# An encoder trunk on one core: lo weights by an accumulating transfer, transforms by time modulo 4, final norm by 128 tokens

## The chip, the cores and the metric

The kernel runs on one core of a Trainium2 chip. The metric is the device time of one execution in microseconds (us), given as the median of several runs. A profiled execution stands beside it: its span runs from the first to the last instruction that the profiler records, and all times of instructions below are from that one execution. Engines are TensorE (PE, with its weight loads as PEld), VectorE (DVE), ScalarE (ACT), GpSimd (POOL) and SyncE (SP), which here issues transfers only.

## What is computed

A trunk of two layers on 512 tokens of 1024 channels, in float32. Cut to what matters here:

```python
for i in range(DEPTH):                       # 2
    h = rmsnorm(x, norm_mix_g[i])
    p = h @ w_in[i]                          # 1024 -> 2176
    y_a = rglru_mixer(...)                   # 384 channels, linear recurrences
    y_b = window_attention(...)              # 384 channels, 6 heads
    h_fwd, h_bwd = hyena_filters(...)        # depends on the weights alone
    y_c = hyena_mixer(c_u, ...)              # 256 channels
    y = concat(rmsnorm(y_a), rmsnorm(y_b), rmsnorm(y_c))
    x = x + y @ w_out[i]
    x = x + relu(rmsnorm(x) @ w_up[i])**2 @ w_down[i]     # 1024 -> 4096 -> 1024
return rmsnorm(x, final_norm_g)

def hyena_mixer(u, ...):
    x0, x1, v = split(depthwise_conv(u))
    z = v * x1
    y = irfft(rfft(z, 2 * L) * rfft(filt_circ, 2 * L))[:L] + z * bias   # L = 512
    return y * x0
```

## The kernel before

**A planner writes the order.** The program is not emitted as it is written. `Plan.record` collects operations with their inputs and outputs; `Plan.schedule` then plays a list schedule with a cost for each operation, and `Plan.issue` emits each engine's instructions in the order that came out. An operation recorded on `nc.any` goes to VectorE or GpSimd, one recorded with `plan.either` to whichever of the named engines is free. Tiles come from pools with a fixed number of buffers (`wraw` 6, `whi` 3, `wlo` 3, `sp` 69, PSUM 7), and an operation is placed only when its tiles have buffers. Where TensorE would have nothing to do, `filler` puts in a small bf16 matmul on constants (written to the tile `wk`), of which nothing is read. As the emission is by a helper, most instructions bear line 456 or 1459, and rows are told apart by tiles.

**Weights.** All products of weights run as three float32r matmuls (`mm3`): a weight is split into a rounded part hi and the rest lo, and the activations likewise, and hi*hi, hi*lo and lo*hi are added. `emit_weight` (line 588) takes the weights in the order `wseq`: SP loads 512 KB into a raw buffer (`load`, line 553, which waits until the third weight before is split), and `split_weight` (line 542) makes hi by a rounding copy and lo by a subtraction on VectorE or GpSimd. `weight` (line 610) keeps LA = 2 weights ahead (4 for the down weights).

**Stages.** For each layer: the input projection by 17 tiles (`pin`), with the recurrence's gates, the attention's units and the transforms between them in the order of the script of the layer (`SCRIPTS`, line 30; numbers are input tiles, F the filters, G the gates, R and U the attention, H the Hyena mixer, S the scan, N and O the group norms and output projections); the output projection (`po`); then the MLP in 8 quads: four tiles of the up projection (`pu`, 24 matmuls each) and, one quad later, the down projection by seven products (`pX`, `pY`, `pZ`, 12 matmuls each), each followed by VectorE's update of x.

**Transforms.** Transforms of length 1024 are matmuls with tables of cosines and sines of half-integer frequencies, split by even and odd time. `load_trig` (line 734) loads six tables of 128x512 and splits each. `dft` (line 755) is 12 float32r matmuls of 256 columns; `filters` (line 765) calls it 4 times, and so does `hyena` (line 1121) for its signal; then come products by frequency (Y), sums (G, split into hi and lo) and the inverse, 48 float32r matmuls of 256 columns.

**End.** The final norm (line 1297) runs by halves of 256 tokens: mean square, power -1/2 on GpSimd, x scaled in place, 16 transposes (`fin`), eight scaled copies out of PSUM, and eight stores of 128 KB by SP.

Of the kernel before, what the change touches and what calls it, by code (L numbers as in the profile page):

```python
# [10 lines left out]
F32 = mybir.dt.float32  # L11
# [158 lines left out]
class Plan:  # L170
# [112 lines left out]
    def schedule(self):  # L283
# [31 lines left out]
        while pending:  # L315
            moved = True
            while moved:
                moved = False
                for e in engines:
# [76 lines left out]
                    if o.dma:  # L396
                        dma_free = max(dma_free, t + 1.0) + c
                        free_at[e] = t + 0.45
                        end = dma_free + 1.2
                    else:  # L400
                        end = t + c
                        free_at[e] = end
                    if LOCK and (e == "gpsimd" or e == "vector" and self.two_port(o)):
                        port_free = end
# [55 lines left out]
def encoder_kernel(ctx, tc, xT, w_in, w_out, w_up, w_down, gates, fw, par, trig, rope, decay, zemb, ident_d, maskb_d, yT):  # L460
# [81 lines left out]
    def split_weight(raw, n, c, hi, lo):  # L542
# [4 lines left out]
        nc.any.tensor_tensor(out=lo[:, :n], in0=raw[:, :n], in1=hi[:, :n].bitcast(F32), op=ALU.subtract)  # L547
# [40 lines left out]
    def emit_weight(key):  # L588
# [10 lines left out]
        else:  # L599
# [5 lines left out]
            out = split_weight(raw, 1024, 128 if kind in ("in", "up") else 512, wtile(whi, F32R, "wh"), wtile(wlo, F32R, "wl"))  # L605
# [4 lines left out]
    def weight(key):  # L610
        n = wseq.index(key)
        la = LA if key[0] != "down" else LA + 2
# [142 lines left out]
    def dft(tabs, src, out):  # L755

        th, tl = [t.rearrange("p (c k) -> p c k", c=2) for t in tabs]
        sh, sl = [t.rearrange("p (c k) -> p c k", c=2) for t in src]
        for kt in range(2):
            o = out[:, kt * 256:(kt + 1) * 256]  # L760
            for c in range(2):
                ks = slice(kt * 128, kt * 128 + 128)
                mm3(o, th[:, c, ks], tl[:, c, ks], sh[:, c, :], sl[:, c, :], c == 0, c == 1)

    def filters(i, tr):
# [15 lines left out]
        for par_ in range(2):  # L781
# [14 lines left out]
            hs.append(split(s, "hs"))  # L796
            hd.append(split(d, "hd"))
        H = {}
        for nm, tb, src in (("c", (0, 4), hs), ("s", (1, 5), hd)):
            pe = PMX("He")  # L800
            dft(tr[tb[0]], src[0], pe)
            e = Fs("e")
            nc.scalar.copy(out=e, in_=pe)
            po = PMX("Ho")
            dft(tr[tb[1]], src[1], po)
            for sg, op in (("+", ALU.add), ("-", ALU.subtract)):
                H[nm + sg] = Fs("H" + nm + ("p" if sg == "+" else "m"))
                nc.vector.tensor_tensor(out=H[nm + sg], in0=e, in1=po, op=op)
        return H
# [28 lines left out]
    nc.any.tensor_scalar(out=hbias, in0=pcols(_cols["ba"][0], _cols["bx"][1]), scalar1=0.5, scalar2=1.0, op0=ALU.mult, op1=ALU.mult)  # L838
    nc.any.tensor_scalar(out=nsink, in0=pcols(*_cols["sink"]), scalar1=-1.0, scalar2=1.0, op0=ALU.mult, op1=ALU.mult)
    nc.any.tensor_scalar(out=s_, in0=lam, scalar1=-1.0, scalar2=1.0, op0=ALU.mult, op1=ALU.mult)  # L840
    nc.vector.tensor_tensor(out=ex, in0=lam, in1=s_, op=ALU.min)
    act(ex, ex, AF.Exp)
    nc.any.tensor_scalar(out=s2, in0=ex, scalar1=2.0, scalar2=1.0, op0=ALU.add, op1=ALU.mult)
    nc.vector.reciprocal(out=s2, in_=s2)
    nc.any.tensor_tensor(out=s_, in0=ex, in1=s2, op=ALU.mult)
    nc.any.tensor_tensor(out=s2, in0=s_, in1=s_, op=ALU.mult)
    nc.any.memset(pl, 2.0 / 17.0)
    for q in range(7, -1, -1):
        nc.any.tensor_tensor(out=pl, in0=pl, in1=s2, op=ALU.mult)
        nc.any.tensor_scalar(out=pl, in0=pl, scalar1=2.0 / (2 * q + 1), scalar2=1.0, op0=ALU.add, op1=ALU.mult)  # L850
    nc.any.tensor_tensor(out=pl, in0=pl, in1=s_, op=ALU.mult)
    nc.vector.tensor_scalar(out=s_, in0=lam, scalar1=-1.0, scalar2=0.0, op0=ALU.mult, op1=ALU.max)
    nc.any.tensor_tensor(out=pl, in0=pl, in1=s_, op=ALU.add)
    nc.any.tensor_scalar(out=m4sp, in0=pl, scalar1=-4.0, scalar2=1.0, op0=ALU.mult, op1=ALU.mult)
    nc.any.tensor_scalar(out=p4sp, in0=pl, scalar1=4.0, scalar2=1.0, op0=ALU.mult, op1=ALU.mult)
# [8 lines left out]
    for i in range(DEPTH):  # L864
# [256 lines left out]
        def hyena(H, tr):  # L1121
# [5 lines left out]
            for par_ in range(2):  # L1127
                p = PMX("zt")
                for c in range(2):
                    for n in range(2):  # L1130
                        src = v[n].rearrange("p (c s two) -> p c two s", c=2, two=2)[:, c, par_, :]
                        nc.tensor.transpose(p[:, c * 256 + n * 128:c * 256 + n * 128 + 128], src, ident)
                zt.append(split(p, "zt"))
            X = {}
            for nm, tb in (("c", (0, 4)), ("s", (1, 5))):
                pe = PMX("Xe")
# [327 lines left out]
```

## Time and profile before

| | |
|---|---|
| median of 3 runs | 1119.79 us (1119.63 to 1120.64) |
| profiled execution, its own time | 1119.31 us |
| its span | 1117.5 us |
| instructions | 14124 |
| TensorE / VectorE / ScalarE / GpSimd busy | 99% / 81% / 53% / 20% |

The busy time of TensorE holds the fills of `wk`, and matmuls overlap: the duration of one is longer than the distance to the next. What a matmul costs in a full stream is the distance between starts.

### The profile page before, as it was taken

What the parts mean: (1) busy time and instruction counts of PE and PEld (TensorE: products, weight loads), DVE (VectorE), ACT (ScalarE), POOL (GpSimd) and SP (SyncE); (2) the same over time, 40 slices, a digit from 0 to 9 for tenths busy, and PEclk for the clock granted to TensorE, in tenths of its full rate; (3) what the DMA queues carried; (4) which work ended last, traced back from release to release, by engine and by line L of the source; (5) the groups of instructions that cost most, each with busy time, mean ns of one, the idle gap of its engine ahead of it and who ended that gap; (6) DMA issues with size and microseconds to landing.
All of it is one profiled execution on the core that took longest, in us unless ns stands there. A gap on an engine that the chain in (4) does not pass through costs nothing. (4 is left out here: it accounts for less than half of the span.)

```text
span 1117.5 us, 14124 instructions
## 1 busy us (share of the span) xinstructions
PE 1105.6 (99%) x5224; PEld 900.1 (81%) x5224; DVE 901.8 (81%) x1374; ACT 587.5 (53%) x958; POOL 229.1 (20%) x143
## 2 busy tenths in 40 slices
PE   9999999999999999999999999999999999999997
PEld 6688788888888688888888888788888888888886
DVE  8999996568797886886989899685597797797796
ACT  6477664365345454344456836644554455355444
POOL 0221422301011131100332242242010111011032
PEclk9999999999999999999999999999999999999999
DMA  9424201221442412422252221022232431341312
GB/s 346 178 76 151 76 1 38 77 95 38 132 132 71 151 57 94 133 75 96 75 185 89 75 75 58 7 70 95 76 98 69 135 116 55 132 132 53 118 57 76
DMA packets 35132, 107.90 MB, mean 97 GB/s; under 512 B 4150, under 2 KB 6710, under 8 KB 35064
## 3 DMA queue, kind: packets, MB, share of 16 engines
q1 hardware_dynamic: 35064, 107.01, 29.1%
q8 instruction: 41, 0.67, 0.2%
q14 instruction: 27, 0.22, 0.1%
HBM read 104.90 MB, written 2.10 MB: 96 GB/s over the span
## 5 line engine op out<-in xcount | busy, mean ns | idle before, releaser
L456 ACT CAST wh<-wr 128x1024 fp32r<-128x1024 f32 x197 | 207.4, 1054 | 347.7 <-PE pu L456 133.8
L456 DVE TENSOR_TENSOR wl<-wr,wh 128x1024 fp32r<-128x1024 f32 (+1 forms) x171 | 213.5, 1251 | 133.2 <-ACT wh L456 129.2
L456 PE MATMUL pu<-xgh,wh 128*128 128x512 f32 x512 | 199.4, 389 | 0.1
L456 PE MATMUL pu<-xgh,wl 128*128 128x512 f32 x512 | 199.4, 390 | 0.0
L456 PE MATMUL pu<-xgl,wh 128*128 128x512 f32 x512 | 199.3, 389 | 0.0
L456 POOL TENSOR_TENSOR wl<-wr,wh 128x1024 fp32r<-128x1024 f32 x56 | 135.5, 2421 | 248.6 <-ACT wh L456 205.9
L456 PEld LDWEIGHTS pu<-xgh,wl 128*128 128x128 f32 x512 | 96.1, 188 | 21.4 <-issue 1.6
L456 PEld LDWEIGHTS pu<-xgh,wh 128*128 128x128 f32 x512 | 96.1, 188 | 20.2 <-ACT xgh L456 0.5
L456 PEld LDWEIGHTS pu<-xgl,wh 128*128 128x128 f32 x512 | 96.1, 188 | 19.9
L456 PE MATMUL pin<-xgh,wl 128*128 128x512 f32 x272 | 107.2, 394 | 0.0
L456 PE MATMUL pin<-xgl,wh 128*128 128x512 f32 x272 | 107.1, 394 | 0.0
L456 PE MATMUL pin<-xgh,wh 128*128 128x512 f32 x272 | 107.1, 394 | 0.0
L456 POOL TENSOR_TENSOR s<-s,h 128x256 f32<-128x256 f32 x12 | 8.9, 743 | 397.3 <-ACT wh L456 388.4
L456 DVE TENSOR_TENSOR wr<-wr 128x1024 f32<-128x1024 f32 x61 | 72.8, 1218 | 0.0
L456 PEld LDWEIGHTS pin<-xgl,wh 128*128 128x128 f32 x272 | 51.1, 188 | 12.1 <-DVE xgl L456 1.9
L456 PEld LDWEIGHTS pin<-xgh,wh 128*128 128x128 f32 x272 | 51.1, 188 | 12.0 <-DVE wl L456 0.8
L456 PEld LDWEIGHTS pin<-xgh,wl 128*128 128x128 f32 x272 | 51.1, 188 | 11.7 <-issue 1.3
L456 DVE SCALAR_TENSOR_TENSOR x<-po,tr,x 128x512 f32<-128x512 f32 x48 | 35.2, 747 | 25.4 <-PE po L456 16.8
L456 PE MATMUL po<-wh,ygh 128*128 128x512 f32 x128 | 51.6, 403 | 0.0
L456 PE MATMUL po<-wh,ygl 128*128 128x512 f32 x128 | 50.7, 396 | 0.0
L456 PE MATMUL po<-wl,ygh 128*128 128x512 f32 x128 | 50.3, 393 | 0.0
L456 DVE SCALAR_TENSOR_TENSOR x<-pY,r,x 128x512 f32<-128x512 f32 x64 | 45.5, 744 | 4.9 <-PE pY L456 4.9
(312 smaller groups left out, 2377.9 us busy)
## 6 DMA issues: line engine op xcount, KB each, us to landing
wr<-in_w_up SPq DMA_DIRECT2D x64, 512.0 KB, 3.5
wr<-in_w_down SPq DMA_DIRECT2D x64, 512.0 KB, 4.3
wr<-in_w_in SPq DMA_DIRECT2D x33, 512.0 KB, 3.7
wr<-in_w_out SPq DMA_DIRECT2D x16, 512.0 KB, 3.5
x<-in_xT SPq DMA_DIRECT2D x16, 256.0 KB, 5.2
dec<-in_decay SPq DMA_DIRECT2D x8, 256.0 KB, 6.3
out_y<-fin SPq DMA_DIRECT2D x16, 128.0 KB, 1.8
traw<-in_trig SPq DMA_DIRECT2D x6, 256.0 KB, 4.1
```

The costliest lines, as they stand in the source:

```text
L456: getattr(getattr(nc, o.eng), o.name)(*[res(a) for a in o.args], **{k: res(v) for k, v in o.kw.items()})
```

## The change

The lo part of an up weight is made without a subtraction on VectorE or GpSimd: lo is first written as the negated rounded weight (ScalarE or VectorE), and a transfer issued on GpSimd's queue adds the raw words onto it. The transforms take time modulo 4 instead of modulo 2: four tables of 128x512 in place of six, unsplit; `sums` makes two float32 matmuls of 256 columns, `spectrum` combines their sums and differences, and the inverse is 16 float32 matmuls of 128 columns on combined inputs U. The final norm runs by 128 tokens: a matmul with the diagonal matrix of the scales takes the place of the scaling and the transposes, and each block is stored with two transfers of 256 KB. Besides: new scripts, LA = 3, `whi` 4, `wlo` 5, `sp` 63, the load waits for the fourth weight before, the parameters of the gates are computed at the first gate instead of ahead of all, and the planner's cost of a transfer on GpSimd's queue.

```diff
-    "8 10 F 3 1 9 0 G0 2 12 G2 G1 7 6 11 R 16 15 I 4 U 5 14 U S 13 H U U U U U NC OC A U NA OA NB OB",
-    "16 1 6 G1 2 14 0 15 G2 8 G0 11 13 12 7 H 10 9 R U 5 U 4 U NC U U U S 3 U OC U A NA OA NB OB",
+    "9 8 F 10 0 2 1 G0 12 G2 11 7 6 4 G1 R U U 16 U 14 15 I U 13 S H U U NC U 5 3 OC U A NA NB OA OB",
+    "16 6 2 14 1 G1 0 11 G2 15 G0 8 13 12 7 H 10 9 R 3 5 U 4 U U U NC U S U U OC A NA U NB OA OB",
-LA = 2
+LA = 3
...
                     if o.dma:
-                        dma_free = max(dma_free, t + 1.0) + c
-                        free_at[e] = t + 0.45
+                        soft = e == "gpsimd"
+                        dma_free = max(dma_free, t + 1.0 + soft) + c * (1 + soft)
+                        free_at[e] = t + (1.0 if soft else 0.45)
...
-    whi = pool("whi", 3, reserve=3)
-    wlo = pool("wlo", 3, reserve=3)
-    sp = pool("sp", 69, reserve=RESERVE)
+    whi = pool("whi", 4, reserve=4)
+    wlo = pool("wlo", 5, reserve=5)
+    sp = pool("sp", 63, reserve=RESERVE)
...
-    def split_weight(raw, n, c, hi, lo):
+    def split_weight(raw, n, c, hi, lo, by_dma=False):
...
-        nc.any.tensor_tensor(out=lo[:, :n], in0=raw[:, :n], in1=hi[:, :n].bitcast(F32), op=ALU.subtract)
+        if by_dma:
+
+            plan.either(
+                ("scalar", "activation", dict(out=lo[:, :n], in_=raw[:, :n], func=AF.Copy, scale=-1.0)),
+                ("vector", "tensor_scalar", dict(out=lo[:, :n], in0=raw[:, :n], scalar1=-1.0, scalar2=None, op0=ALU.mult)),
+            )
+            nc.gpsimd.dma_start(out=lo[:, :n].bitcast(F32), in_=raw[:, :n], accum_op=ALU.add)
+        else:
+            nc.any.tensor_tensor(out=lo[:, :n], in0=raw[:, :n], in1=hi[:, :n].bitcast(F32), op=ALU.subtract)
...
-        if len(wdone) >= 3:
-            plan.extra = {wdone[-3]}
+        if len(wdone) >= 4:
+            plan.extra = {wdone[-4]}
...
-        la = LA if key[0] != "down" else LA + 2
+        la = LA if key[0] != "down" else LA + 1
...
-            raw = Fs("traw")
-            nc.sync.dma_start(out=raw, in_=trig[n])
-            tr[n] = split(raw, "trig")
+            tr[n] = Fs("trig")
+            nc.sync.dma_start(out=tr[n], in_=trig[n])
...
+    def sums(tab, par, src, name):
+
+        p, b = PMX(name), Fs("b")
+        for c in range(2):
+            q, h = par + 2 * c, slice(c * 256, c * 256 + 256)
+            nc.tensor.matmul(out=p[:, h], lhsT=tab[:, q * 128:q * 128 + 128], rhs=src[:, h], start=True, stop=True)
+        nc.scalar.copy(out=b[:, :256], in_=p[:, 256:512])
+        return p[:, :256], b[:, :256]
+
+    def spectrum(tr, even, odd, name):
...
+        for nm, tab in (("c", 0), ("s", 1)):
+            a, b = sums(tr[tab], 0, even[tab], name + "e")
+            comb(e[nm][:, lo], a, b, ALU.add)
+            comb(e[nm][:, hi], *((a, b) if nm == "c" else (b, a)), ALU.subtract)
+        for nm, tab in (("c", 0), ("s", 1)):
+            for n in range(2 if odd[0] is not odd[1] else 1):
+                src = odd[tab] if n == 0 else odd[1 - tab]
+                a, b = sums(tr[tab], 1, src, name + "o")
+                if n == 0:
+                    comb(o[nm][:, lo], a, b, ALU.add)
+                if n == 1 or odd[0] is odd[1]:
+                    comb(o["s" if nm == "c" else "c"][:, hi], a, b, ALU.subtract)
+        for nm in "cs":
+            for sg, op in (("+", ALU.add), ("-", ALU.subtract)):
+                out[nm + sg] = Fs(name + nm + ("p" if sg == "+" else "m"))
+                nc.any.tensor_tensor(out=out[nm + sg], in0=e[nm], in1=o[nm], op=op)
+        return out
...
-                zt.append(split(p, "zt"))
...
+                z = Fs("zt")
+                rounded(z, p)
+                zt.append(z)
+            X = spectrum(tr, [zt[0], zt[0]], [zt[1], zt[1]], "X")
...
-                    G[nm, pr] = split(g, "G")
+                    G[nm, pr] = g
...
+                    nc.any.tensor_tensor(out=U[nm, pr][:, lo], in0=a[:, lo], in1=b[:, hi], op=ALU.add if plus else ALU.subtract)
+                    nc.any.tensor_tensor(out=U[nm, pr][:, hi], in0=a[:, lo], in1=b[:, hi], op=ALU.subtract if plus else ALU.add)
...
+                for q in range(4):
+                    o = p[:, q * 128:q * 128 + 128]
+                    c = (q // 2) * 256 + n * 128
+                    for k, nm in enumerate("cs"):
+                        nc.tensor.matmul(out=o, lhsT=U[nm, q % 2][:, c:c + 128], rhs=tr[2 + k][:, q * 128:q * 128 + 128], start=k == 0, stop=k == 1)
...
-    for h in range(2):
+    for t in range(4):
         plan.prio = -0.5
...
+        r = token_rstd((t,))
+        d = Fs("diag")
+        nc.vector.tensor_scalar(out=d[:, :128], in0=ident, scalar1=r[:, 0:1], scalar2=1.0, op0=ALU.mult, op1=ALU.mult)
+        for n in range(2):
+            p, y = PMX("fin"), Fs("fin")
+            y.parts = True
+            for k in range(4):
+                c = slice(k * 128, k * 128 + 128)
+                nc.tensor.matmul(out=p[:, c], lhsT=x[t][n][:, c], rhs=d[:, :128], start=True, stop=True)
...
+            nc.sync.dma_start(out=yT[4 * n:4 * n + 4, :, t * 128:t * 128 + 128].rearrange("k p c -> p k c"), in_=y.rearrange("p (k c) -> p k c", k=4))
```

## Rows read from the trace of the kernel before

**Rows 1.** Page, part 1: busy us of each engine, share of the span, instructions.

```profile
PE 1105.6 (99%) x5224; PEld 900.1 (81%) x5224; DVE 901.8 (81%) x1374; ACT 587.5 (53%) x958; POOL 229.1 (20%) x143
```

**Rows 2.** Busy by stage: length, busy us (records) by engine; granted clock; DMA share, GB/s.

```profile
20.00:60.00 40.00, 39.18 (x156) 28.09 (x155) 38.42 (x69) 18.74 (x25) 9.25 (x8) 1.00 0.59 213
...
120.00:170.00 50.00, 47.33 (x313) 38.09 (x311) 48.66 (x98) 36.00 (x88) 15.88 (x12) 1.00 0.10 32
...
227.00:565.00 338.00, 337.97 (x1521) 275.93 (x1520) 268.15 (x374) 160.09 (x222) 52.79 (x30) 1.00 0.30 99
...
640.00:700.00 60.00, 58.76 (x340) 48.67 (x339) 57.15 (x101) 29.84 (x62) 21.18 (x16) 1.00 0.19 63
...
772.00:1104.40 332.40, 332.37 (x1487) 274.62 (x1486) 261.51 (x356) 164.61 (x231) 50.77 (x27) 1.00 0.28 91
```

**Rows 3.** The same view for the tile wk alone (fills).

```profile
0.00:20.00 20.00, 7.77 (x42) 1.00 0.93 332
...
120.00:170.00 50.00, 5.13 (x41) 1.00 0.10 32
...
227.00:565.00 338.00, 5.77 (x45) 1.00 0.30 99
...
640.00:700.00 60.00, 2.52 (x17) 1.00 0.19 63
...
772.00:1104.20 332.20, 1.49 (x9) 1.00 0.28 91
...
sum 1117.50, PE 26.90; mean PE 2.69
```

**Rows 4.** Timeline of PE, a forward transform: start us, us, engine, line, operation.

```profile
147.14 0.28 PE L456 MATMUL Xe<-zth,trigh 128*128 128x256 f32 x1
147.26 0.28 PE L456 MATMUL Xe<-ztl,trigh 128*128 128x256 f32 x1
```

**Rows 5.** Timelines of PE, merged neighbours: attention's pv, last transposes.

```profile
156.31 2.10 PE L456 MATMUL pv<-pth,vt 128*128 128x384 f32 x6
...
1110.00 1.94 PE L456 MATMUL fin<-ident,x 128*128 128x128 f32 x16 [0.15 <-DVE x L456]
```

**Rows 6.** Page, part 5: groups; x count | busy us, mean ns of one | idle before.

```profile
L456 ACT CAST wh<-wr 128x1024 fp32r<-128x1024 f32 x197 | 207.4, 1054 | 347.7 <-PE pu L456 133.8
L456 DVE TENSOR_TENSOR wl<-wr,wh 128x1024 fp32r<-128x1024 f32 (+1 forms) x171 | 213.5, 1251 | 133.2 <-ACT wh L456 129.2
...
L456 POOL TENSOR_TENSOR wl<-wr,wh 128x1024 fp32r<-128x1024 f32 x56 | 135.5, 2421 | 248.6 <-ACT wh L456 205.9
```

**Rows 7.** Page, part 6: transfers; count, KB each, median us from issue to landing.

```profile
wr<-in_w_up SPq DMA_DIRECT2D x64, 512.0 KB, 3.5
...
out_y<-fin SPq DMA_DIRECT2D x16, 128.0 KB, 1.8
```

**Rows 8.** Timeline, end of a fill in layer 0's MLP.

```profile
457.23 0.19 PEld L456 LDWEIGHTS pY<-wh,sah 128*128 128x128 f32 x1 [0.18 <-DVE x L456]
```

**Rows 9.** Timeline of the end, all engines.

```profile
1104.44 0.75 DVE L456 SCALAR_TENSOR_TENSOR x<-pY,r,x 128x512 f32<-128x512 f32 x1 [0.34 <-PE pY L456]
...
1106.16 0.61 ACT L456 ACTIVATE sq<-x 128x512 f32<-128x512 f32 x1
...
1107.12 7.92 SPq L456 DMA_DIRECT2D out_y<-fin  x16
...
1108.62 0.71 POOL L456 TENSOR_TENSOR tr<-ms,mhalf 128x2 f32<-128x2 f32 x1 [2.94 <-DVE ms L456]
...
1110.88 1.70 DVE L456 TENSOR_SCALAR fin<-fin,pall 128x256 f32<-128x256 f32 x4 [0.63 <-PE fin L456]
```

**Rows 10.** Groups of VectorE by tile: count | busy us, mean ns of one.

```profile
L456 DVE TENSOR_TENSOR s<-s,h 128x256 f32<-128x256 f32 x52 | 22.5, 432 | 0.1
...
L456 DVE TENSOR_TENSOR rs<-rs,ropet 128x512 f32<-128x512 f32 x4 | 7.5, 1871 | 0.0
...
L456 DVE TENSOR_TENSOR G<-t,t 128x512 f32<-128x512 f32 x8 | 5.1, 676 | 0.0
```

More of the change, by code (lines that the diff above doesn't have):

```diff
@@ L604, in emit_weight @@
                 load(raw, {"in": w_in, "up": w_up}[kind][i, key[2]] if kind != "out" else w_out[i, key[2]])
-            out = split_weight(raw, 1024, 128 if kind in ("in", "up") else 512, wtile(whi, F32R, "wh"), wtile(wlo, F32R, "wl"))
+            out = split_weight(raw, 1024, 128 if kind in ("in", "up") else 512, wtile(whi, F32R, "wh"), wtile(wlo, F32R, "wl"), kind == "up")
         wdone.append(len(plan.ops) - 1)
@@ L753, in sin_stage, with comb @@
         act(out, aa, AF.Sin)
[L755 to L763, printed above, removed]
+    def sums(tab, par, src, name):
[6 more added lines that the diff above has]
+    def spectrum(tr, even, odd, name):
+        lo, hi = slice(0, 256), slice(256, 512)
+        def comb(out, a, b, op):
+            nc.vector.tensor_tensor(out=out, in0=a, in1=b, op=op)
+        out = {}
+        e, o = {}, {}
+        for nm, tab in (("c", 0), ("s", 1)):
+            e[nm], o[nm] = Fs("e"), Fs("o")
+        for nm, tab in (("c", 0), ("s", 1)):
+            a, b = sums(tr[tab], 0, even[tab], name + "e")
+            comb(e[nm][:, lo], a, b, ALU.add)
+            comb(e[nm][:, hi], *((a, b) if nm == "c" else (b, a)), ALU.subtract)
+        for nm, tab in (("c", 0), ("s", 1)):
+            for n in range(2 if odd[0] is not odd[1] else 1):
[10 more added lines that the diff above has]
+        return out
     def filters(i, tr):
@@ L795, in filters @@
                 nc.any.tensor_tensor(out=d[:, cs], in0=f[:, 0:256], in1=f[:, 256:512], op=ALU.subtract)
[L796 to L809, printed above, removed]
+            hs.append(s)
+            hd.append(d)
+        return spectrum(tr, [hs[0], hd[0]], [hs[1], hd[1]], "H")
     def conv(i, u, taps, wname, bname, j, nj, centre):
@@ L843, in encoder_kernel @@
[L843 to L850, printed above, removed]
@@ L1130, in hyena @@
                     for n in range(2):
-                        src = v[n].rearrange("p (c s two) -> p c two s", c=2, two=2)[:, c, par_, :]
+                        src = v[n].rearrange("p (r four) -> p four r", four=4)[:, par_ + 2 * c, :]
                         nc.tensor.transpose(p[:, c * 256 + n * 128:c * 256 + n * 128 + 128], src, ident)
-                zt.append(split(p, "zt"))
-            X = {}
-            for nm, tb in (("c", (0, 4)), ("s", (1, 5))):
-                pe = PMX("Xe")
-                dft(tr[tb[0]], zt[0], pe)
-                e = Fs("e")
-                nc.scalar.copy(out=e, in_=pe)
-                po = PMX("Xo")
-                dft(tr[tb[1]], zt[1], po)
-                for sg, op in (("+", ALU.add), ("-", ALU.subtract)):
-                    X[nm + sg] = Fs("X")
-                    nc.vector.tensor_tensor(out=X[nm + sg], in0=e, in1=po, op=op)
+                z = Fs("zt")
+                rounded(z, p)
+                zt.append(z)
+            X = spectrum(tr, [zt[0], zt[0]], [zt[1], zt[1]], "X")
             Y = {}
@@ L1191, in encoder_kernel @@
             elif step[0] == "G":
+                if i == 0 and not lru_st:
+                    gate_parameters()
                 lru_gates(int(step[1]))
```

86 lines of the change are left out of this document (40 added, 46 removed).

## Prediction

> **What bounds the kernel now.** I read the page's busy shares first: TensorE is busy in 99% of the span [rows 1]. That share has to be cleaned before it can be used, since where nothing is ready the planner fills TensorE with small bf16 matmuls that compute nothing (wk). So next the busy time of each engine by stage [rows 2], then the same view for the tile wk alone [rows 3]. Together: 26.9 us of the span are such fills; outside them, and outside the first 20 us and the tail, TensorE is never idle for long. In layer 1's MLP (772 to 1104 us) 1.5 us of 332 are fills, the granted clock is 1.00 (2.4 GHz), and so every matmul removed is time removed. Two stages are different. In layer 0's mixing VectorE is as full as TensorE: 38.4 of 40 us and 48.7 of 50 us [rows 2], and there the fills are 5.1 us; layer 1's mixing (640 to 700 us) has 57.2 of 60 us and 2.5 us of fills. Layer 0's MLP has 5.8 us of fills although VectorE is only 79% busy; the one I followed ends with VectorE's update of x, which frees a product's bank [rows 8]: VectorE was late in its own order.
>
> **Part 1, the Hyena transforms (fewer, dearer matmuls).** Before, each forward transform is 4 calls of `dft` of 12 matmuls with 256 columns in float32r; two transforms in each of two layers give 192, and the inverse gives 48 a layer, 96. Neighbours start 0.12 us apart [rows 4], so 288 x 0.12 = 34.6 us of TensorE. After, they are float32 matmuls. The trace has such a matmul in attention: `pv`, 384 columns, 40 calls in the code and 80 records, so two records a call. Six in a row take 2.10 us, the last 0.49 of it being its own length: (2.10 - 0.49)/5 = 0.322 us a record [rows 5]. By columns that is 0.215 us a record for 256, 0.43 us a matmul. For 128 columns it would be 0.107; the float32 transposes of the final norm, which load new weights for every 128 columns, start (1.94 - 0.27)/15 = 0.111 us apart [rows 5], which I take. So: filters 12 matmuls, 5.2 us a layer; `spectrum` of the signal 8, 3.4 us; inverse 16 of 128 columns, 16 x 0.222 = 3.6 us. Two layers: 24.4 us. **TensorE loses 10.2 us**; from both sides, with the 128-column ones at 0.12 a record and 0.107, 9.6 to 10.4. The strided transposes stay 16.
>
> What it does to VectorE matters where that engine is full. Removed per layer: lo parts of zt (2), hs/hd (4) and G (4) and 8 sums out of PSUM, 18 passes of 512 columns at about 0.68 us [rows 10], 12.2 us, and in layer 0 also 6 lo parts of the trig tables, 4 us. Added: 16 half-width passes in the two `spectrum` calls and 8 for U at 0.43 us [rows 10], 10.3 us, and 8 full sums, 5.4 us: 15.8 us. (Half of all these may run on GpSimd.) So VectorE gains 0.5 us in layer 0 and loses 3.6 us in layer 1: no relief to speak of, and a longer chain (matmul, ScalarE copy, combination, sum) through it. I therefore book 9.3 of the 10.2 us; the bounds are 4 (all of the X and y share of layer 0 and part of layer 1's lost to VectorE) and 10.4.
>
> **Part 2, lo of the up weights.** A lo part is one two-input pass now: 1.25 us on VectorE, 2.42 on GpSimd [rows 6]. For 64 of 227 weights it becomes a scaled copy (the cast beside it on ScalarE takes 1.05 us [rows 6]; on VectorE it would be less than 1.25) and a transfer issued by GpSimd. If the up weights are as evenly shared as all are (171 to 56), VectorE loses 48 passes, 60 us, and GpSimd 16, 39 us; ScalarE, 160 of 338 us busy in layer 0's MLP [rows 2], takes up to 34 us a layer and stays off the path. That relief is worth something only where VectorE was late: of the 5.8 us of fills in layer 0's MLP I book **3.0 us**; bounds 0 and 5.8. In layer 1's MLP there is nothing to win.
>
> The transfer itself is not in the trace. From below: a load of 512 KB lands in 3.5 us [rows 7]. From above: it reads two operands, so two such loads, and the issue on GpSimd as long as its costliest pass, 2.4 us: 9.4 us. I take 6, nearer to the load, as the same 16 engines do it and are 70% idle there (share 0.30 and 0.28, [rows 2]). What hides it: a down product is 12 matmuls and an up tile 24. Layer 1's MLP has 1487 records, 9 of them fills, so (332.4 - 1.5)/1478 = 0.224 us a matmul [rows 2, 3], 2.7 us a product and 5.4 us an up tile. With 5 lo buffers the first up tile of a quad gets its buffer when the fifth weight before it is done: four products, 10.8 us, less 1.05 for the copy: 9.7 us of cover. Later tiles of the quad have more. At 6 us: **cost 0**; at 9.4 still 0, with nothing to spare. Behind the transfer on GpSimd's queue stand a few shared sums; the raw buffer is held longer, so SP's next load waits longer, also inside that cover.
>
> First the row, then a rule that speaks against this part. In this trace a two-input VectorE pass (rs) takes 1.87 us on average where its like take 0.68 [rows 10], which I read as GpSimd, busy beside it, holding it up. The Trainium skill, "SBUF — State Buffer", section "SBUF: two separate sides", says that a transfer issued from GpSimd can't write its descriptors while VectorE runs a copy or scale of SBUF data with both ports; its example goes from about 620 to 3100 ns. By the row the cover holds and the sum stays; by that example, as an estimate, the transfer takes 2.5 us more, and only at its upper bound would that outlast the cover and make the first rival true.
>
> **Part 3, final norm by 128 tokens.** Now the last update of x ends at 1104.44 + 0.75 = 1105.2; its square waits for ScalarE until 1106.16, its power on GpSimd comes at 1108.6, transposes at 1110.0, and SP, which issued 16 stores one by one, ends its last issue at 1107.1 + 7.9 = 1115.0 [rows 9, 5]; an issue is 7.92/16 = 0.5 us, so that one began at 1114.5, lands 1.8 later [rows 7] at 1116.3, and 1.2 us close the span. After, the last token block needs: square 0.6, three small VectorE passes (mean, diagonal), each under the 0.43 of a half-width one [rows 10], together 0.9, power 0.7, 16 records x 0.111 = 1.8, a last scaled copy 1.70/4 = 0.4, hops between engines 0.6 (an estimate), one issue 0.5, landing 1.8 to 2.5 (a store twice the size) and the 1.2: 8.5 to 9.2 us after 1105.2, so 1113.7 to 1114.4 against 1117.5. Against that stand the float32 products: 64 records instead of 32 transposes; those of the first block, 1.8 us, may be put ahead of the last down product. Gain 1.3 to 3.8, **booked 2.5 us**.
>
> **Part 4, order and buffers.** New scripts keep two input tiles (5 and 3; 3 in layer 1 much earlier) for the end of layer 0's mixing, where TensorE ran dry between 120 and 170 us [rows 3]; whi 3 to 4, wlo 3 to 5, sp 69 to 63 (the trig tables need 8 tiles fewer). Of the 5.1 + 2.5 us of fills in both mixing stages and a few us of late starts I book **3.0 us**; bounds -4 (a worse order) and 8. The gate parameters leave the start: the 7.8 us of fills there [rows 3] wait for the first x and its lo parts; booked 0, at best 1.
>
> **Sum.** 9.3 + 3.0 + 2.5 + 3.0 = 17.8 us. The profiled execution took 1119.3 us (span 1117.5 and 1.8 around it): 1101.5. The median of the runs is 0.5 above it: **1102 us**.
>
> **Rivals.** (a) *The transfer comes late.* One mechanism: with L us from issue to landing over 9.7, TensorE waits at the first up tile of each quad but the first, 14 times. It decides from L = 9.7 + 17.8/14 = 11.0 us. The upper bound of 9.4 with one GpSimd pass of 2.4 us queued ahead [rows 6] makes 11.8, and 14 x 2.1 = 29 us: 1131. For: no row has the transfer, and the upper bound lies at the edge. Against: 3.5 us for the load, idle transfer engines. Chance 0.10, all of it slower, at 1118 to 1140. (b) *VectorE is the bound of mixing.* Part 1 gives 4, part 2 only 2, part 4 nothing or a loss: 1119.8 - 4 - 2 - 2.5 = 1111, between 1108 and 1119. For: 97% busy between 120 and 170 us; against: GpSimd is at 32% in that stage and can take sums. Chance 0.15. (c) *Relief closes the gaps.* All fills of both mixings and of layer 0's MLP go, and part 1 counts in full: 1119.8 - 10.4 - 13.4 - 4 = 1092. Chance 0.15, 1086 to 1096. (d) *It doesn't do what it says*: if the accumulated transfers replace no VectorE time on the path, part 2 is 0 and the time 1105: inside the forecast.
>
> **How the numbers follow.** Forecast 0.60, 1096 to 1108. The range leaves out (a) and the bottom of (c) and takes in (b): 1091 to 1117. This kernel can tell a change of about 0.2%, 2.2 us. Slower: (a) and a little of (b), 0.11; within: the top of (b), 0.03; faster 0.86.
>
> **What would show it.** Fewer records of X, H and y, at 0.215 and 0.111 us apart (part 1); wl passes down by 64 and, in the MLP stages, fills near zero with VectorE under 75% (part 2); last landing within 9 us of the last x update (part 3); fills between 100 and 230 us under 4 us (part 4). Wrong would be: fills or idle time ahead of pu, released by a transfer (a); VectorE still full and fills in mixing unchanged (b).

## The result and the profile after

The changed kernel takes 1130.05 us (median of 4 runs, 1129.87 to 1130.28) beside 1120.22 for the kernel before in the same session: ratio 1.0083, 95% interval 1.0067 to 1.0099. It is slower by some 9 us (9.8 between these medians, 9.3 by the ratio) where 18 us less were forecast. The profiled execution took 1130.3 us, its span 1128.5 against 1117.5.

The page's first part for the kernel after, to be read against [rows 1]:

```profile
PE 1110.4 (98%) x5188; PEld 900.7 (80%) x5188; DVE 867.4 (77%) x1357; ACT 620.4 (55%) x998; POOL 252.4 (22%) x213
```

VectorE has 34 us less to do, and TensorE is "busy" for 5 us longer. By stages, in the columns of [rows 2]:

```profile
20.00:60.00 40.00, 38.29 (x154) 29.27 (x154) 38.18 (x64) 17.39 (x24) 13.77 (x13) 0.96 0.59 215
120.00:170.00 50.00, 50.00 (x259) 38.98 (x257) 43.21 (x88) 25.66 (x68) 12.44 (x11) 1.00 0.30 106
227.00:565.00 338.00, 337.54 (x1492) 275.21 (x1491) 249.10 (x355) 184.38 (x251) 70.91 (x61) 1.00 0.53 144
640.00:700.00 60.00, 56.18 (x283) 45.81 (x282) 59.29 (x84) 25.19 (x39) 18.79 (x12) 1.00 0.23 79
772.00:1104.40 332.40, 332.38 (x1482) 275.25 (x1481) 235.48 (x325) 182.91 (x251) 69.27 (x61) 1.00 0.54 142
```

VectorE's load fell in both MLPs (268 to 249 us and 262 to 235 us), as the change intends. The fills, the tile wk alone, in the columns of [rows 3]; two stretches are added that were empty before (0.00 us in each):

```profile
0.00:20.00 20.00, 8.36 (x41) 1.00 0.91 326
60.00:120.00 60.00, 11.53 (x101) 1.00 0.09 28
120.00:170.00 50.00, 1.80 (x12) 1.00 0.30 106
227.00:565.00 338.00, 1.55 (x11) 1.00 0.53 144
640.00:700.00 60.00, 2.27 (x20) 1.00 0.23 79
700.00:770.00 70.00, 9.10 (x75) 1.00 0.09 27
...
0.00:1128.50 1128.50, 36.03 (x264) 1.00 0.44 125
```

The fills have moved and grown: 36.0 us instead of 26.9. Those of 120 to 170 us and of layer 0's MLP shrank as hoped; 11.5 and 9.1 us stand where there were none. What TensorE and ScalarE do around the largest one:

```profile
104.07 3.67 PE L457 MATMUL wk<-warmc 128*128 128x256 bf16 x32
...
109.15 7.59 PE L457 MATMUL wk<-warmc 128*128 128x256 bf16 x68
116.57 0.60 PE L457 MATMUL pt<-ident,e 128*128 128x128 f32 x4
...
106.90 0.45 ACT L457 ACTIVATE e<-s,mn 128x256 f32<-128x256 f32 x1
...
108.55 1.28 ACT L457 ACT_TABLE_LOAD   x1
109.85 0.63 ACT L457 ACTIVATE tg<-tg 128x512 f32<-128x512 f32 x1
...
110.78 2.69 ACT L457 ACTIVATE tg<-tg 128x512 f32<-128x512 f32 x5
113.49 1.28 ACT L457 ACT_TABLE_LOAD   x1
...
114.90 0.46 ACT L457 ACTIVATE e<-s,mn 128x256 f32<-128x256 f32 x1
```

Attention's first exponentials run at 106.9 us; then ScalarE loads another function table, takes the six square roots of the scan (tg), loads the first table back, and only at 114.9 comes to the next unit's exponentials. TensorE has nothing ready from 109.15 to 116.57. In the kernel before, the first exponentials came after the square roots, with input tiles to multiply meanwhile.

A ledger, worked out from the traces, sets the runs side by side. It sums the distance from each TensorE record's start to the next one's, by what the record computes, so that a wait counts with the product ahead of it (us; a fill's column differs a little from its busy time for that reason):

| kernel | transforms | fills | input tiles (pin) | final norm | all else | span |
|---|---|---|---|---|---|---|
| before | 37.1 | 25.4 | 191.1 | 3.5 | 860.4 | 1117.5 |
| after | 23.8 | 35.9 | 198.9 | 7.1 | 862.8 | 1128.5 |
| e1 old weights | 23.5 | 28.0 | 197.9 | 7.1 | 860.6 | 1117.1 |
| e4 transforms only | 24.5 | 43.4 | 192.1 | 3.5 | 864.5 | 1128.0 |
| e7 before, 63 tiles | 35.7 | 56.4 | 198.3 | 3.5 | 863.3 | 1157.2 |
| e8 e1, 63 tiles | 23.6 | 36.6 | 197.8 | 7.1 | 862.0 | 1127.1 |
| e10 other order | 24.7 | 22.5 | 198.0 | 7.0 | 857.1 | 1109.3 |
| e11 e10 and transfer | 23.6 | 21.9 | 199.1 | 7.0 | 857.1 | 1108.7 |
| e12 fewer fills | 24.6 | 18.6 | 198.0 | 7.0 | 861.6 | 1109.8 |
| e13 before, other order | 37.1 | 22.6 | 193.1 | 3.5 | 861.1 | 1117.4 |

From before to after: transforms -13.3, fills +10.5, input tiles +7.8, final norm +3.6, the rest +2.4: +11.0. The saved TensorE time is there in full, and was spent again.

What the input tiles gained is mostly waits; 1.7 us of it is a lower clock. TensorE had waited 1.7 us for the filters, and then its granted clock was 0.59 on average over 4 us, most of them at the lower level of 1.2 GHz, with products of 512 columns 0.43 us apart instead of 0.22:

```profile
48.73 1.07 PE L457 MATMUL f<-h,fw 64*64 64x512 f32 x2 [1.71 <-ACT h L457]
...
50.00:54.00 4.00, 4.00 (x12) 3.10 (x12) 3.97 (x8) 1.43 (x2) 0.00 (x0) 0.59 0.37 129
```

That is not what made the kernel slower: one of its four runs had a mean granted clock of 1.0 and took 1130.22 us all the same.

### The profile page after: what moved, and what is told of

It reads as the page before. It is cut to its first block, busy times and chain, and to the rows that moved or that the text cites. A ratio compares the mean times of both kernels' runs of the same rounds, so it can differ in the third digit from the quotient of the medians.

```text
span 1128.5 us, 14270 instructions
## 1 busy us (share of the span) xinstructions
PE 1110.4 (98%) x5188; PEld 900.7 (80%) x5188; DVE 867.4 (77%) x1357; ACT 620.4 (55%) x998; POOL 252.4 (22%) x213
## 4 chain that ended last, share of the span: by engine, by line
PE 83%; DVE 12%; issue 2%; ACT 1%; DMA 1%; POOL 0%; SPq 0%; POOLq 0%; ACTq 0%; DVEq 0%
PE pu L457 31%; PE pY L457 14%; PE pin L457 9%; PE po L457 8%; PE pZ L457 7%; PE pX L457 4%; PE pv L457 2%; DVE wl L457 2%; PE gate L457 2%; PE wk L457 1%; PE s L457 1%; DVE t L457 1%; PE f L457 1%; DVE rq L457 1%; PE xt L457 1%
## 5 line engine op out<-in xcount | busy, mean ns | idle before, releaser
L457 ACT CAST wh<-wr 128x1024 fp32r<-128x1024 f32 x192 | 201.9, 1052 | 260.7 <-PE pu L457 97.7
L457 DVE TENSOR_TENSOR wl<-wr,wh 128x1024 fp32r<-128x1024 f32 (+1 forms) x128 | 159.2, 1245 | 52.3 <-ACT wh L457 51.6
L457 PE MATMUL pin<-xgl,wh 128*128 128x512 f32 x272 | 108.7, 400 | 0.2 <-DVE xgl L457 0.2
L457 POOL TENSOR_TENSOR wl<-wr,wh 128x1024 fp32r<-128x1024 f32 x35 | 84.1, 2403 | 91.8 <-ACT wh L457 82.2
L457 POOL DMA_DIRECT2D wl<-wr x64 | 55.7, 874 | 139.7 <-ACT wl L457 80.1
L457 DVE TENSOR_TENSOR s<-h 128x256 f32<-128x256 f32 x52 | 21.9, 422 | 78.4 <-ACT h L457 78.3
L457 DVE TENSOR_TENSOR wr<-wr 128x1024 f32<-128x1024 f32 x64 | 75.5, 1218 | 0.2
L457 POOL TENSOR_TENSOR s<-h 128x256 f32<-128x256 f32 x12 | 8.8, 736 | 298.5 <-ACT h L457 298.5
L457 ACT ACTIVATE wl<-wr 128x1024 fp32r<-128x1024 f32 x53 | 56.2, 1059 | 33.7 <-PE pY L457 19.2
L457 ACT ACTIVATE relu<-pu 128x512 f32<-128x512 f32 x64 | 37.8, 591 | 55.6 <-PE pu L457 55.6
```

The source lines that it names most:

```text
L457: getattr(getattr(nc, o.eng), o.name)(*[res(a) for a in o.args], **{k: res(v) for k, v in o.kw.items()})
```

## Experiments

The theories. **N**, the prediction's own: TensorE's time in mixing lies on the path. **P** and **O**: the gain was lost by the order of mixing, which the smaller pool of small tiles (sp, 69 to 63) or the weight pipeline displaced. **T** and **V**: the transforms' longer chains, or VectorE in general, set the length of mixing, and TensorE's saving can't come off. **D**: the transfers land late. **S**: two engines that write parts of one output tile take turns. (R and Q, in e11, are told there.)

### e1: the old weight pipeline

```diff
-LA = 3
+LA = 2
-    whi = pool("whi", 4, reserve=4)
-    wlo = pool("wlo", 5, reserve=5)
-    sp = pool("sp", 63, reserve=RESERVE)
+    whi = pool("whi", 3, reserve=3)
+    wlo = pool("wlo", 3, reserve=3)
+    sp = pool("sp", 69, reserve=RESERVE)
-        if len(wdone) >= 4:
-            plan.extra = {wdone[-4]}
+        if len(wdone) >= 3:
+            plan.extra = {wdone[-3]}
-            out = split_weight(..., kind == "up")
+            out = split_weight(..., False)
-        la = LA if key[0] != "down" else LA + 1
+        la = LA if key[0] != "down" else LA + 2
```

> The changed kernel with the weights as before: lo by a subtraction on VectorE or GpSimd, 3 hi and 3 lo buffers, 69 small tiles, look-ahead 2; transforms, norm, scripts stay new. Theory P (the weight part upset the order): the deeper weight queue runs ahead of the mixing's own work and this is what opened the fills of 11 us in each attention stretch; here the wk fills of both mixing stages fall from 25 to under 12 us and the time to 1112-1120. Theory T (the transforms: their longer chain through VectorE and ScalarE starves attention): fills stay at 20 us or more, 1125-1133, as the VectorE work of the transforms is unchanged. Theory D (transfers land late in the MLP): the MLP stages, 344.7 and 326.7 us now, get shorter by 5 us or more.

1120.77 us, ratio to before 1.0002 (0.9984 to 1.0019): all 9 us of the loss are gone, 8 us of them from the fills. P's own figures are missed by a little: the two mixing stages keep 17 us of fills, not under 12, and the time lies just above 1120; T, which wanted 1125 us or more, falls for these scripts. The loss sits in the weight part of the change, in the number of its buffers or in its transfer; but the transforms' 13 us still don't show.

### e2: engines subtract, buffers as changed

```diff
-            out = split_weight(..., kind == "up")
+            out = split_weight(..., False)
```

> The changed kernel with lo of the up weights by a subtraction again, but with the 4 hi and 5 lo buffers, 63 small tiles and look-ahead 3 kept. Theory P (buffers and look-ahead upset the order, not the transfer): within 3 us of 1130, fills in both mixings unchanged at about 25 us. Theory D (the accumulating transfer costs): 1120 or less, MLP stages shorter than 344.7 and 326.7 us. Theory T: within 3 us of 1130 too, so this run tells D from the others, and the run with the old weights tells P from T.

1128.48 us, 1.0064 (1.0039 to 1.0089). The transfer isn't what costs the 9 us: without it 1.6 us go, and both mixing stages stay as long. D falls. What is left between e1 and e2 is the weight buffers, the small tiles and loads one weight earlier.

### e3: each final tile by one engine

```diff
-                plan.either(("scalar", "activation", ...), ("vector", "tensor_scalar", ...))
+                if n == 0:
+                    nc.scalar.activation(out=y[:, c], in_=p[:, c], func=AF.Copy, scale=g)
+                else:
+                    nc.vector.tensor_scalar(out=y[:, c], in0=p[:, c], scalar1=g, ...)
```

> The changed kernel; in the final norm the scaled copies of the first half of the channels all go to ScalarE, those of the second half all to VectorE, so that no output tile is written by both. Theory S (two engines writing one tile wait for each other in turn, 0.4 us a copy): the stretch from the last down product to the end falls from 14.8 us to 11.5-12.5, the time to 1127-1128, nothing else moves. Rival (the copies themselves or the power on GpSimd bound the tail): within 0.7 us of 1130.

1127.91 us, 1.0061 (1.0043 to 1.0080); from the last down product to the end 13.0 us instead of 15.0 (13.5 before). The ends, the changed kernel first and this run second:

```profile
1113.73 3.73 PE L457 MATMUL fin<-diag,x 128*128 128x128 f32 x32
...
1113.93 0.75 DVE L457 SCALAR_TENSOR_TENSOR x<-pY,r,x 128x512 f32<-128x512 f32 x1 [0.16 <-PE pY L457]
...
1119.00 3.84 PE L457 MATMUL fin<-diag,x 128*128 128x128 f32 x32 [1.43 <-DVE ms L457]
...
1122.03 0.63 ACT L457 ACTIVATE fin<-fin,pall 128x128 f32<-128x128 f32 x2 [0.42 <-DVE fin L457]
1122.43 0.61 DVE L457 TENSOR_SCALAR fin<-fin,pall 128x128 f32<-128x128 f32 x2 [0.44 <-ACT fin L457]
```

```profile
1113.08 7.31 PE L457 MATMUL fin<-diag,x 128*128 128x128 f32 x64
```

In the first, ScalarE waits 0.42 us for VectorE's copy and VectorE 0.44 for ScalarE's, in turn, though they write different parts of the tile fin, and TensorE stops for 1.43 us. In the second the 64 records run through: 2 us of the tail, a little less than S expected. The edit gives each engine a PSUM tile to read as well as an output tile to write, so it isn't shown which of the two made them take turns, nor whether the chip or the program's own synchronization by tile did.

### e4: the transforms alone, in the old order

The kernel before with the new tables, `load_trig`, `sums`, `spectrum` and inverse, and its own scripts, weights, gate parameters and norm. The core:

```diff
-                dft(tr[tb[0]], zt[0], pe)
...
+            X = spectrum(tr, [zt[0], zt[0]], [zt[1], zt[1]], "X")
...
-                            mm3(o, gh[:, c, ch], gl[:, c, ch], th[:, c, :], tl[:, c, :], q == 0, q == 3)
+                        nc.tensor.matmul(out=o, lhsT=U[nm, q % 2][:, c:c + 128], rhs=tr[2 + k][:, q * 128:q * 128 + 128], start=k == 0, stop=k == 1)
```

> The kernel before with the new transforms alone (time modulo 4 in float32, unsplit tables); weights, scripts, norm, gate parameters as before. Forecast's own step (TensorE's 10.2 us come off the time): 1110-1113. Theory T (the transforms starve attention): fills in the mixing stages of 15 us or more against 7.6 before, 1120 or more although TensorE has 10 us less to do.

1128.08 us, 1.0060 (1.0039 to 1.0081). The transforms are 12.6 us shorter on TensorE and the kernel is 7 us slower. The stretch of 120 to 170 us of this run, wk alone:

```profile
120.00:170.00 50.00, 16.54 (x149) 0.90 0.10 32
```

16.5 us of fills against 5.1 [rows 3], and a granted clock of 0.90. What the largest fill stands ahead of:

```profile
147.44 3.12 PE L457 MATMUL Xe<-zt,trig 128*128 128x256 f32 x8
...
157.17 14.35 PE L457 MATMUL wk<-warmc 128*128 128x256 bf16 x130
171.36 3.74 PE L457 MATMUL y<-trig,U 128*128 128x128 f32 x32
```

It stands ahead of the inverse, whose inputs U VectorE finishes at 168.6 us, after sums, products by frequency and combinations one behind the other. From the first product of X to the first of y this layer needs 171.36 - 147.44 = 23.9 us; in the kernel before it was 161.30 - 146.35 = 15.0, with no fill ahead of y. So in the old order the longer chain (T) is what TensorE waits for. e1, with the same transforms and new scripts, has other work to put there and is as fast as before.

### e5: short products, old order

```diff
+    def narrow(o, *names):
+        o.kw = dict(o.kw, **{n: o.kw[n][:, :16] for n in names})
-        nc.tensor.matmul(out=out, lhsT=lh, rhs=rl, start=False, stop=False)
-        nc.tensor.matmul(out=out, lhsT=ll, rhs=rh, start=False, stop=stop)
+        narrow(nc.tensor.matmul(out=out, lhsT=lh, rhs=rl, ...), "out", "rhs")
+        narrow(nc.tensor.matmul(out=out, lhsT=ll, rhs=rh, ...), "out", "rhs")
```

> The kernel before, each instruction in its old place in its engine's order; of the three products of each transform the two with a low part run over 16 columns instead of 256 (a part of the low-order terms is left out). It takes 160 products of 0.16 us down to some 0.05 us, about 17 us of TensorE time, 11 in layer 0's mixing (its filters among them) and 6 in layer 1's, and leaves ScalarE, VectorE and GpSimd as they are. Theory N (the prediction's own: TensorE's time in mixing lies on the path): 1103 to 1108 us. Theory V (VectorE and the chains between the engines set the length of mixing, TensorE waits anyway): 1114 us or more, layer 0's mixing still over 217 us, and the fills grow by most of what was taken.

1128.28 us, 1.0076 (1.0057 to 1.0094): slower, which neither theory said. The experiment didn't take the time that it meant to: 192 products of 0.12 us were cut, not 160 of 0.16. Its timeline of PE, and its stretches by engine:

```profile
62.86 0.17 PE L456 MATMUL He<-hdl,trigh 128*128 128x16 f32 x1
62.89 0.26 PE L456 MATMUL He<-hdh,trigl 128*128 128x16 f32 x1
63.00 0.36 PE L456 MATMUL He<-hdh,trigh 128*128 128x256 f32 x1
63.20 0.17 PE L456 MATMUL He<-hdl,trigh 128*128 128x16 f32 x1
...
68.10 0.63 PE L456 MATMUL pin<-xgl,wh 128*128 128x512 f32 x1
68.53 0.63 PE L456 MATMUL pin<-xgh,wl 128*128 128x512 f32 x1
...
60.00:80.00 20.00, 20.00 (x98) 17.13 (x97) 17.30 (x29) 12.16 (x19) 1.28 (x1) 0.83 0.25 79
...
640.00:700.00 60.00, 59.09 (x285) 50.70 (x283) 51.60 (x74) 25.82 (x38) 17.43 (x11) 0.86 0.18 62
```

A group of three products takes 63.20 - 62.86 = 0.34 us, where three full ones take 3 x 0.12 = 0.36 [rows 4]: each still loads its own weights, and these loads start 0.11 to 0.12 us apart (at 62.74, 62.86, 62.97 and 63.08 us). And the granted clock falls, to 0.83 and 0.86 on average in stretches where before it was 1.00 [rows 2]; the 512-column products behind the short ones start 0.43 us apart instead of 0.22. The run decides nothing between N and V, but shows that in this order fewer columns on TensorE can cost time by themselves.

### e6: short taps, old order

```diff
-            nc.vector.scalar_tensor_tensor(out=o[:, do], in0=u[:, di], ..., in1=o[:, do], ...)
+            q = nc.vector.scalar_tensor_tensor(out=o[:, do], in0=u[:, di], ..., in1=o[:, do], ...)
+            q.kw = dict(q.kw, **{a: q.kw[a][:, :16] for a in ("out", "in0", "in1")})
```

> The kernel before, each instruction in its old place in its engine's order; the convolutions' taps after the first run over 16 columns instead of some 511 (the rest of the taps is left out). It takes 21 VectorE instructions per layer from 0.81 us to some 0.1 us: 15 us of VectorE in layer 0's mixing and about as much in layer 1's, and leaves TensorE as it is. Theory V: layer 0's mixing falls by 7 us or more from 221.9, the whole to 1112 us or less. Theory N (TensorE bounds mixing, VectorE's full rows are work that others wait for little): 1117 us or more, layer 0's mixing within 3 us of 221.9.

1117.19 us, 0.9973 (0.9963 to 0.9984). Layer 0's mixing, 20 to 227 us, before and then this run:

```profile
20.00:227.00 207.00, 203.51 (x1039) 163.11 (x1038) 181.45 (x307) 120.43 (x235) 53.18 (x37) 1.00 0.28 96
```

```profile
20.00:227.00 207.00, 204.27 (x1049) 164.76 (x1048) 173.64 (x310) 122.15 (x239) 54.69 (x37) 1.00 0.28 98
```

VectorE's busy time fell by 7.8 us here (15 were meant: a short tap costs more than 0.1 us) and by 19 us over the span; the whole gained 3, layer 0's mixing 1.9 and layer 1's nothing. That is within what N expected; V, as a bound by VectorE's amount of work, is not supported. One reservation: an order that is fixed keeps its fills, so relief can shorten only open waits here.

### e7 and e8: 63 small tiles

```diff
-    sp = pool("sp", 69, reserve=RESERVE)
+    sp = pool("sp", 63, reserve=RESERVE)
```

The one line in the kernel before (e7), and in e1 (e8).

> The kernel before with one number changed: 63 small tiles instead of 69, the count that the change leaves. Same instructions, same work. Theory O (the fewer small tiles that the change pays its weight buffers with displace the order of mixing): 1128 us or more, the loss in the mixing stages, the MLPs unchanged within 2 us. Rival (the count of tiles is a reserve, and what cost the time are the transforms' chains or the added weight buffers): 1118 to 1122 us.

> The run with the old weight pipeline (new transforms, scripts and norm; 3 and 3 weight buffers; engines subtract; 1120.8 us, 28.0 us of fills) with one number changed: 63 small tiles instead of 69. Theory O (the six small tiles that pay for the weight buffers are what the change loses by): 1127 us or more, fills over 34 us, the mixing stages longer and the MLPs as they are. Rival (the loss belongs to the added weight buffers and their earlier loads; the tile count did harm only in the kernel before, whose scripts were made for 69): 1119 to 1123 us.

e7: 1157.40 us, 1.0331 (1.0313 to 1.0348). e8: 1129.06 us, 1.0077 (1.0060 to 1.0094). In both it is the mixing stages that grow, and in e7 layer 0's MLP by 7.5 us too, against the expectation. The PE timeline of e8:

```profile
103.33 3.67 PE L457 MATMUL wk<-warmc 128*128 128x256 bf16 x32
108.39 7.59 PE L457 MATMUL wk<-warmc 128*128 128x256 bf16 x68
```

These are the two large fills of the changed kernel, record for record (x32, x68), in a kernel with the old weight buffers, the old loads and no transfer. So six small tiles fewer are enough for 8.3 of the 9.3 us that the change's weight part costs. The reverse, the added buffers with 69 small tiles, wasn't run.

What is missing there shows beside e1. The starts of its twelfth and thirteenth input tile (24 products each), then that of e8's thirteenth:

```profile
102.16 0.48 PE L457 MATMUL pin<-xgh,wh 128*128 128x512 f32 x1
...
113.16 0.47 PE L457 MATMUL pin<-xgh,wh 128*128 128x512 f32 x1
```

```profile
117.34 0.68 PE L457 MATMUL pin<-xgh,wh 128*128 128x512 f32 x1
```

In e1 exponentials and square roots alternate on ScalarE as well (tables loaded at 104.1, 106.4 and 108.7 us), but TensorE has the twelfth input tile to multiply from 102.2 to 109.5. In e8 the last product of the twelfth starts at 103.1 and the thirteenth comes only at 117.3: between them stand the fills.

### e9, e10, e12, e13: other orders

The steps of the two scripts moved among their neighbours; e9 with 3 and 3 weight buffers and 69 tiles, e10 and e12 with 4 and 4, 65 tiles and loads three ahead, all with the final copies of e3; e13 is the kernel before in an order found with the same effort.

Layer 0's script of e10 against that of the changed kernel:

```diff
-    "9 8 F 10 0 2 1 G0 12 G2 11 7 6 4 G1 R U U 16 U 14 15 I U 13 S H U U NC U 5 3 OC U A NA NB OA OB"
+    "9 8 F 10 0 2 1 G2 G0 12 11 6 7 G1 R 4 U U 16 U 15 14 I U 13 S H U U NC U 3 5 OC U A NA NB OA OB"
```

> New transforms and norm with the old weight pipeline and 69 small tiles as in the run at 1120.8 us, the final copies each output tile by one engine, and the steps of mixing in another order (both scripts changed by some moves of neighbours). Its program holds 142 fills where that of before holds 188 and that of the changed kernel 264. Theory O with the prediction's own term (the transforms' saved TensorE time is real, and the order decides whether it comes off the end or goes into fills): fills 20 us or less, 1107 to 1114 us. Rival (the transforms' saved time can't come off, since VectorE or the chains set the length of mixing): 1117 us or more, with waits in place of the fills.

> The same with 4 and 4 weight buffers, 65 small tiles and loads three weights ahead, in an order of its own (155 fills in its program; engines subtract). Theory O: the added weight buffers do no harm by themselves where the order suits 65 tiles: 1107 to 1114 us, like the run beside it. Rival (weight buffers and earlier loads cost time): 1118 us or more.

> The run at 1111.45 us in one more order of its mixing steps, whose program holds 121 fills instead of 155. Theory O (the time goes with TensorE's transform work plus the fills that the order needs): 34 fills of some 0.13 us are 4.5 us: 1105 to 1109 us. Rival (fewer fills become open waits or a lower clock, as in the run with 142 fills, where a stretch at 1.2 GHz took some of it back): 1110 to 1114 us.

> The kernel before with its old transforms, weights and norm, and only its mixing steps in another order, found with the same effort as the order of the run at 1111.45 us; its program holds 167 fills instead of 188. Theory O with the prediction's term (the transforms' saved 13 us are real, and an order that suits them brings them off the end): the old transforms gain little by any order, 1115 to 1121 us. Rival (what made the run at 1111.45 us fast is the order alone, not the transforms): 1113 us or less.

e9: 1114.85 us, 0.9946 (0.9924 to 0.9967), 0.9 us above O's range, its runs spread from 1111.6 to 1117.5; in the profiled one, of 1117.5, the granted clock was 0.68 between 60 and 80 us. e10: **1111.45 us**, 0.9915 (0.9901 to 0.9930). e12: 1112.64 us, 0.9930 (0.9914 to 0.9947): 3.9 us of fills fewer than e10 in the ledger and 4.5 us more in "all else"; waits around attention's pv and the output projection took their place (2.0 and 1.7 us), as its rival said. e13: 1119.42 us, 0.9985 (0.9974 to 0.9997). So the order alone, in the one that was tried, is worth 1.4 us to the old transforms, while the new ones, in an order that suits them (e10), come out 8 us faster than that, 0.5 of it from the tail: the transforms' saving can come off the end, and e10's added weight buffers do no harm.

### e11: the transfer, in e10's order

```diff
-            out = split_weight(..., False)
+            out = split_weight(..., kind == "up")
```

> The run at 1111.45 us (4 and 4 weight buffers, 65 small tiles, its own order) with one thing added: the up projection's lo weights come by negation and the accumulating transfer, as in the changed kernel. Its program holds 153 fills against 155, so the order is nearly the same. Theory R (the prediction's: the relief of VectorE in layer 0's MLP comes off the end): 1107 to 1109 us. Theory Q (the MLP is bound by TensorE once its fills are gone, so the relief is worth nothing and the transfer costs its late landings): 1111 to 1114 us, layer 0's MLP not shorter than 343.5.

**1110.10 us**, 0.9901 (0.9886 to 0.9916), the fastest: all four parts of the change, with 65 tiles and four lo buffers, its own order and one engine for each final tile. Its runs (1109.35 to 1110.56) lie 1.3 us under e10's (1111.04 to 1112.09); layer 0's MLP is 342.5 us instead of 343.5. That lies between what R and Q expected, and the intervals of the two ratios overlap, so the 1.3 us lean on runs of two sessions. Its rows: fills in two stretches and over the whole, and what TensorE waited for in layer 1's mixing and between 20 and 60 us.

```profile
60.00:120.00 60.00, 4.15 (x35) 1.00 0.18 61
...
700.00:770.00 70.00, 0.27 (x1) 1.00 0.26 70
...
0.00:1108.70 1108.70, 22.23 (x153) 1.00 0.44 127
...
PE y L457 <- DVE U L457: 1.6, 1, 1.6
PE zt L457 <- DVE cv L457: 1.5, 1, 1.5
...
PE f L457 <- ACT h L457: 1.7, 1, 1.7
```

## Why the prediction was wrong, step by step

**Part 1, TensorE's own time: right.** The rows of the changed kernel, the view of one tile and a merged timeline:

```profile
L457 PE MATMUL Xe<-zt,trig x8: 377/379/382, 655.8 to 657.3; 128*128 128x256 f32 x8
```

```profile
684.43 2.84 PE L457 MATMUL y<-trig,U 128*128 128x128 f32 x24
```

Eight starts in 1.5 us are 0.214 us each, and (2.84 - 0.28)/23 = 0.111: as taken from [rows 5]. 24.4 us were computed and 23.8 measured. Before, 34.6 were computed and the ledger has 37.1, since it holds waits of 2.5 us; the saving is 13.3, over the 10.2.

**Part 1, what of it comes off the end: wrong.** 9.3 of 10.2 were booked, so 0.9 for the longer chain through VectorE. e1 differs from before by parts 1 and 3, the scripts and the place of the gate parameters: +0.1 us against the before of its session, and part 3 alone cost 1.5, so part 1 with its scripts was worth 1.4. From the first product of X to the first of y layer 0 needs 171.81 - 152.22 = 19.6 us in the changed kernel and 23.9 in e4, where it was 15.0 before; other work of VectorE falls into that time too, but in e4 it is this chain that TensorE fills 14 us for. In the best order a part of it still shows, the 1.6 us that TensorE waits for VectorE's U. Two other waits of that run stand ahead of the new transforms, in work that the change left as it was: 1.5 us for the convolution ahead of zt, and 1.7 for the filters, where it was 0.8 before. The ledger's input tiles, with which such waits count, hold some 7 us more in every row that has the new transforms and new scripts. The lower bound of 4 was nearer, for a reason that was named and then priced by VectorE's amount of work instead of by the length of the chain.

**Part 2: the cover held, the relief was worth little.** Page after, transfers and the issue on GpSimd:

```profile
wl<-wr POOLq DMA_DIRECT2D x64, 512.0 KB, 8.1
...
L457 POOL DMA_DIRECT2D wl<-wr x64 | 55.7, 874 | 139.7 <-ACT wl L457 80.1
...
L457 PE MATMUL pu<-xgh,wl 128*128 128x512 f32 x512 | 199.7, 390 | 0.4 <-DMA wl<-wr 0.4
```

8.1 us from issue to landing, between the bounds of 3.5 and 9.4 (6 was taken, and e11's median is 6.0); TensorE waited 0.4 us for it in all, so rival (a) didn't come. VectorE's passes fell by 43, not 48, and layer 0's MLP lost most of its fills (5.8 to 1.6 us). But the step from VectorE's load to those 5.8 us failed: in e4, with the old weights, the same stage has 0.27 us of fills. They went with the order and needed no relief of VectorE. The transfer's own worth is some 1.6 us lost in the changed kernel's order (e2, with intervals that overlap) and 1.3 us gained in e11's; 3.0 was booked. By the example that the prediction cited from the Trainium skill, "SBUF — State Buffer", section "SBUF: two separate sides", a transfer held up by a copy on VectorE would take some 2.5 us more, as an estimate. The trace shows no such hold-up, but is a weak test of it: the planner starts no such pass beside an issue (`LOCK`), and the three that ran beside one all the same, for some 0.6 us, landed after 6.7 to 7.5 us.

**Part 3: wrong by one term.** The end comes 1128.5 - 1114.7 = 13.8 us after the last update of x, not within 9. The sum had 16 records behind that update, 1.8 us; all 64, 7.1 us, run behind the last down product, since none was put ahead of it. The turns of the two engines add 2 us, which the rows of before don't show. With these gone (e3) the tail is 13.0 us against 13.5: 0.5 us instead of 2.5.

**Part 4: wrong in sign, and the step that decides.** 3.0 us were booked, with -4 as the worse bound. The weight part of the change, its buffers, its tiles and at most 1.6 us of transfer, costs 1130.05 - 1120.77 = 9.3 us; six small tiles alone cost 8.3 (e8). The prediction took them as free, "the trig tables need 8 tiles fewer". The planner passes over an instruction whose output finds no free tile, so the count of tiles is part of the order; the fills between 120 and 170 us did fall, and larger ones came up elsewhere. The place of the gate parameters, booked at 0, gave nothing at the start either: 8.4 us of fills in the first 20 us instead of 7.8.

**The rivals.** (b) forecast fills in mixing unchanged because VectorE is full; they grew, and taking 19 us off VectorE gave 3. (c) has its time nowhere. None of the four was "the order gets worse", although its bound stood in part 4.

Against the forecast, the 28 us between 1102 and 1130 are about 15 from the weight part (a gain of 3.0 booked in part 2 and 3.0 in part 4, a loss of 9.3 measured), 8 from part 1 with its scripts (9.3 booked, 1.4 measured) and 4 from part 3 (a gain of 2.5 booked, a loss of 1.5 measured). Such shares are estimates, since what one part costs depends on the order that the others leave.

**Left open.** Why the thirteenth input tile comes late with 63 small tiles, that is, which of them is missing first, wasn't followed. Nor is it shown how much of the 7 us among the input tiles goes with the chain's length and how much with the scripts: e4, in the old order, has fills instead, and e7 has as much there with the old transforms.

## What to carry to other kernels

Where a planner fills in waits and hands out buffers, a change of buffer counts is a change of order: run the count alone first, and read the fills by stretch, not their sum. Time that is taken off the busiest engine comes off the end only in an order made for it, so give the new kernel the same search for an order that the old one had, and give the old one that search too. A chain that grows longer is to be priced by its steps and hops, even where each engine on it gains time.

## What the runs showed of the hardware

- A float32r product of 16 columns with 128x128 weights doesn't cost a sixteenth of one of 256: three of which two were short took 0.34 us instead of 0.36 (e5).
- With short products the granted clock fell, to 0.83 and 0.86 on average in stretches of 20 and 60 us (e5), and this cost more than the work that was left out. In the changed kernel it was 0.59 over 4 us behind a wait of 1.7 us, and in e9 0.68 over 20 us, which wasn't followed.
- An accumulating transfer of 512 KB between two tiles lands in 6.0 us (e11) to 8.1 us (the changed kernel), by the median, where a load of that size takes 3.5, and occupies GpSimd for 0.87 us.
- ScalarE and VectorE, reading parts of one PSUM tile and writing parts of one output tile, took turns and waited 0.42 to 0.44 us at each change; what makes them do so isn't shown.
- The prediction's reading of the slow rs pass [rows 10] holds: in the kernel before, the three long ones (2.0 to 2.4 us) started within a subtraction of 2.4 us on GpSimd and ended 0.55 us after it; the fourth, with GpSimd idle, took 0.67 us.
